# A hybrid decoder block on one core: low parts of weights, transposes and head copies given to other places

## The chip, the cores and the metric

The kernel runs on one core of one Trainium2 chip. The metric is the device time of one execution in microseconds (us). TensorE is called PE (PEld where it loads weights), VectorE DVE, ScalarE ACT, GpSimd POOL, SyncE SP. A `q` behind an engine's name (ACTq, SPq) is that engine's queue of DMA issues and semaphore instructions.

## What is computed

One layer for 512 tokens of width 1024, all in float32:

```python
h = rmsnorm(x, norm1_g);  proj = h @ w_in
u, v_g, q, k, v, q_idx, k_idx, w_idx, gates = split_cols(proj, IN_SIZES)
y_a = sgu_mixer(gelu(u), gelu(v_g), w_s, b_s, sgu_ln_g, sgu_ln_b)   # chunked gMLP
q, k, q_idx, k_idx = apply_rope(...)
y_b = dsa_attention(q, k, v, q_idx, k_idx, w_idx)  # 128 best keys of each query, 8 heads
merged = sigmoid(g0) * (y_a @ w_out_a) + sigmoid(g1) * (y_b @ w_out_b)
x = x + merged @ w_o
x = x + square(relu(rmsnorm(x, norm2_g) @ w_ff_in)) @ w_ff_out
return rmsnorm(x, norm_f_g)
```

The gMLP multiplies `u` by a spatially mixed, layer-normed `v_g`; the product is what the code holds in `u` after line 562, and its transpose `yaT` is the input of `y_a @ w_out_a`.

## The kernel before, in words

**Split products.** Each float32 matmul is three matmuls in a faster format: every operand is kept as a rounded high part and a low part (the rest). `split` (line 50) makes them: ACT writes the high part (line 51), and DVE, or the engine handed in, subtracts (line 52). A step of `gemm` (line 140) is one 128-row slice of the contraction: low weight by high input, high by low, high by high (lines 146 to 148).

**Weights** come in tiles of 128x1024 through `w_load` (line 102; issued from ACT's queue, two raw buffers `wr`) and `w_conv` (line 109), which makes `wh` on ACT and `wl` on the engine in `lo_eng["e"]`, three buffers each, and then issues the load of the next tile. That issue has to wait until both parts of an earlier tile have been made, since they free the raw buffer. `w_ahead(n)` is called after the first step of weight tile n and converts up to tile n+2. `lo_eng["e"]` is POOL from line 316 on and DVE again from line 529 on.

**Order.** The program writes TensorE's work as generators: a list `todo` of gemms, from which `fill(n)` takes n steps and which it places among the work of the other branches; what has to be done with a finished sum is put off by `later` to the next `tick`. A planner of the framework then orders each engine's queue by its own estimate of when operands are ready, with the program's order as priority; instructions within `tc.keep_in_program_order` keep their place. So most of the order is the program's, and some is the planner's.

**The stages around the change.** DVE searches the 128 best keys (lines 517 to 521: 16 rounds of MAX8 and MATCH_REPLACE8 over three score tiles) and after that makes masks (line 526). Below this, PE runs gate sums `ga`, and then the projection of the keys of heads 0 to 3 (`k`, tiles W_K0, 16 steps, line 551). Between its steps stand the four spatial mixes `sg` (lines 559 to 561), of which DVE makes the gated product `u` (line 562, one instruction for each of the four groups). Then comes the projection of the queries of heads 0 to 3 (`q`, tiles W_Q0, 16 steps, line 565), and after each of the first four of its steps one group of four transposes of `u` (line 570), which ACT copies (line 571) and DVE subtracts from (line 572) to `yaT` high and low. Then `oa`, the product with `w_out_a` (line 581, 30 steps by `fill(30)`), and then the heads.

**Head copies.** `rope` (line 328) turns the `k` or `q` sums by eight DVE instructions in all (lines 333 to 336) and two ACT copies. `k_done` and `q_done` (lines 541, 546) then call `restack` (line 349), which copies 32-row pieces to the layout of each of four heads `hh`: 32 copies for the keys, 16 for the queries, 64 KB each, all issued from SP's queue. A second round of the same copies serves heads 4 to 7 (lines 697, 698). Attention runs through `Block.scores` (lines 620, 621, tile `at`), `normalise`, `transpose` (tile `pt`) and `values` (tile `pv`), with `fill` putting steps of other sums between. The buffers `kq` of heads 2 and 3 are used again by heads 6 and 7.

Of the kernel before, what the change touches and what calls it, by code (L numbers as in the profile page):

```python
# [15 lines left out]
P = 128  # L16
# [17 lines left out]
def hybrid_block_kernel(ctx: ExitStack, tc: tile.TileContext, A: dict, out: bass.AP):  # L34
    nc = tc.nc
    ACT, DVE, POOL, PE = nc.scalar, nc.vector, nc.gpsimd, nc.tensor
# [7 lines left out]
    def bank(name, tag="ps"):  # L44
        return ps.tile([P, 512], F32, tag=tag, bufs=4, name=name)

    def f32(ap):
        return ap.bitcast(F32)
# [6 lines left out]
    def unit(tag, dt, name):  # L55
        bufs = dict(kq=6, T=3)[tag]
        return E.tile([P, 2, S], dt, tag=tag, bufs=bufs, name=name)
# [11 lines left out]
    def tick():  # L69
        for d in due:  # L70
            d[0] -= 1
        while due and due[0][0] <= 0:
            due.pop(0)[1]()
# [4 lines left out]
    def fill(n):  # L78
        while n > 0 and todo:
            try:  # L80
                next(todo[0])
                n -= 1
                tick()
            except StopIteration:
                todo.pop(0)
# [14 lines left out]
    lo_eng = dict(e=DVE)  # L100
# [39 lines left out]
    def gemm(dst, get, ah, al, evac, lag=1, t0=0):  # L140

        wh, wl, n = get()
        K = len(ah)
        for k in range(K):
            bh, bl = ah[k][:, t0:], al[k][:, t0:]
            PE.matmul(dst, wl[:, k], bh, start=(k == 0), stop=False)  # L146
            PE.matmul(dst, wh[:, k], bl, start=False, stop=False)  # L147
            PE.matmul(dst, wh[:, k], bh, start=False, stop=(k == K - 1))  # L148
            if k == 0 and n is not None:
                w_ahead(n)  # L150
            if k == K - 1:
                later(evac, lag)
            yield
# [35 lines left out]
    ident = G.tile([P, P], F32, name="ident")  # L189
# [138 lines left out]
    def rope(xy, T, name, t0):  # L328


        for n in range(2):
            a, b = tmp(f"{name}_a{n}")[:, t0:], tmp(f"{name}_b{n}")[:, t0:]
            DVE.tensor_tensor(a, xy[n], cosR[:, t0:], op=ALU.mult)
            DVE.tensor_tensor(b, xy[1 - n], sinR[:, t0:], op=ALU.mult)
            DVE.tensor_tensor(a, a, b, op=ALU.subtract if n == 0 else ALU.add)
            split(T[n], T[2 + n], a)

    def rope_tiles(gets, name, done, t0=0):
        xy = [bank(f"{name}{n}")[:, t0:] for n in range(2)]

        def finish():
            t = [unit("T", FR, f"{name}_T{c}") for c in range(2)]
            T = [t[c][:, d, t0:] for c in range(2) for d in range(2)]
            rope(xy, T, name, t0)
            done(T)
        for n in range(2):
            yield from gemm(xy[n], gets[n], hTh, hTl, finish if n else (lambda: None), t0=t0)

    def restack(dst, T, hh, order):
        for c, o in enumerate(order):  # L350
            nc.sync.dma_start(f32(dst[32 * c:32 * c + 32, :]), f32(T[o][32 * hh:32 * hh + 32, :]))

    def bcast_r():
        pr = bank("pr", "pa")
# [8 lines left out]
    def qi_done(T):  # L363
        for hh in range(4):
            if hh % 2 == 0:
                un = unit("kq", FR, f"QSi{len(QSi)}")
            q = un[:, hh % 2, :S - P]
            restack(q, T, hh, (0, 1, 2, 3))
            QSi.append(q)
# [25 lines left out]
    for n in range(2):  # L395
        b = bank(f"kti{n}", "pa")
# [7 lines left out]
    u, vg = None, None  # L404
# [121 lines left out]
        DVE.tensor_scalar(sc[i], sc[i], TAKEN, -BIG, op0=ALU.is_gt, op1=ALU.mult)  # L526
    while todo:
        fill(8)
    lo_eng["e"] = DVE


    kq = []

    def new_kq():
        kq.clear()
        for hp in range(2):
            un = [unit("kq", FR, f"kq{hp}{c}") for c in range(3)]
            kq.append((un[0][:, 0], un[0][:, 1], un[2][:, 0]))
            kq.append((un[1][:, 0], un[1][:, 1], un[2][:, 1]))

    def k_done(T):
        for hh in range(4):
            restack(kq[hh][1], T, hh, (0, 1, 0, 1))
            restack(kq[hh][2], T, hh, (2, 3, 2, 3))

    def q_done(T):
        for hh in range(4):
            restack(kq[hh][0], T, hh, (0, 1, 2, 3))

    new_kq()  # L550
    todo.append(rope_tiles(W_K0, "k0", k_done))
    fill(12)
    u = dst_uv["u"]
    vgh, vgl = vghl
    yaT = [half("ybt", 2, f"yaT{c}") for c in "hl"]
    for g in range(4):
        b = bank(f"sg{g}", "pa")
        c = slice(g * P, (g + 1) * P)
# [4 lines left out]
                                 u[:, :, c], op0=ALU.add, op1=ALU.mult)  # L563
    fill(4)
    todo.append(rope_tiles(W_Q0, "q0", q_done))
    for g in range(4):
        fill(1)
        b = bank(f"yt{g}", "pa")
        for c in range(NT):
            PE.transpose(b[:, c * P:(c + 1) * P], u[:, c, g * P:(g + 1) * P], ident)  # L570
        ACT.activation(yaT[0][:, g], b, AF.Copy)
        DVE.tensor_tensor(yaT[1][:, g], b, f32(yaT[0][:, g]), op=ALU.subtract)
    while todo:
# [121 lines left out]
    new_kq()  # L695
    flush()
    k_done(ybs["KT"])
    todo.append(rope_tiles(W_Q1, "q1", q_done))
    todo.extend(gate_b(m) for m in range(2, KD))
    fill(27)  # L700
# [433 lines left out]
```

## Time and profile before

| | |
|---|---|
| time, median of 3 runs | 706.39 us (706.03 to 706.98) |
| profiled execution: its own time, its span | 707.55 us, 705.8 us |
| granted TensorE clock, mean | 0.993 |
| busy: PE, PEld | 690.5 us (98%), 578.0 us (82%) |
| busy: DVE, ACT, POOL | 563.0 us (80%), 331.9 us (47%), 67.9 us (10%) |
| instructions | 8976 |

The profile is one execution. Times in it are counted from the start of the span. Busy time of PE is modelled, as matmuls are pipelined: a matmul of 128x512 is shown with 0.39 us, though the next one starts some 0.23 us after it. "Idle before" is what an engine stood still before an instruction, and an arrow names what it waited for.

### The profile page before, as it was taken

The numbers are of one execution on the slowest core, as the hardware profiler recorded it, in microseconds if no ns is written. First come the engines' busy times: TensorE is split into PE (matmuls) and PEld (weight loads), VectorE is DVE, ScalarE is ACT, GpSimd is POOL, SyncE is SP. The second block draws the span as 40 slices with busy tenths as digits, with TensorE's granted clock in tenths as the row PEclk, the third lists the DMA queues.
The fourth block names the chain that finished last, engine by engine and source line by source line (L and its number), as shares of the span: only waits on it lengthen the run. The fifth ranks groups of instructions, "written<-read, shape, count | busy, mean of one in ns | idle before, by whom it ended". The sixth has DMA issues, their size and how long they took to land.

```text
span 705.8 us, 8976 instructions
## 1 busy us (share of the span) xinstructions
PE 690.5 (98%) x3242; PEld 578.0 (82%) x3242; DVE 563.0 (80%) x1036; ACT 331.9 (47%) x572; POOL 67.9 (10%) x49
## 2 busy tenths in 40 slices
PE   9999999996999999999999999999999999999996
PEld 8998888885888887878888888888888888888885
DVE  5674999999557887768542978979798997979996
ACT  6644634413235546563335766445253544535234
POOL 0044348720000000000000000000000000000001
PEclk9999999998999999999999999999999999999999
DMA  9736222313652454214443223242323214233023
GB/s 328 264 95 190 60 90 90 108 42 113 183 155 75 136 143 124 75 46 141 158 154 133 74 99 129 69 150 90 120 92 116 92 59 150 90 119 114 7 61 119
DMA packets 27356, 82.03 MB, mean 116 GB/s; under 512 B 4656, under 2 KB 6320, under 8 KB 25264
## 3 DMA queue, kind: packets, MB, share of 16 engines
q10 hardware_dynamic: 14976, 60.34, 26.6%
q1 hardware_dynamic: 12336, 21.12, 9.5%
q8 instruction: 25, 0.41, 0.2%
q14 instruction: 19, 0.16, 0.1%
HBM read 71.48 MB, written 2.10 MB: 104 GB/s over the span
## 4 chain that ended last, share of the span: by engine, by line
PE 71%; DVE 3%; DMA 1%; SPq 1%; issue 1%; ACT 0%; POOLq 0%; POOL 0%; DVEq 0%; ACTq 0%
PE f L146 8%; PE f L147 8%; PE f L148 8%; PE pp L897 6%; PE pp L898 6%; PE pp L899 6%; PE wo L147 2%; PE wo L148 2%; PE wo L146 2%; PE gb L146 1%; PE gb L148 1%; PE gb L147 1%; PE pv L651 1%; PE pt L639 1%; PE q L146 1%; PE oa L147 1%
## 5 line engine op out<-in xcount | busy, mean ns | idle before, releaser
L51 ACT ACTIVATE wh<-wr 128x1024 fp32r<-128x1024 f32 x88 | 93.0, 1057 | 116.1 <-PE f L148 39.4
L52 DVE TENSOR_TENSOR wl<-wr,wh 128x1024 fp32r<-128x1024 f32 x69 | 83.9, 1218 | 21.4 <-ACT wh L51 19.8
L146 PE MATMUL f<-h2h,wl 128*128 128x512 f32 x256 | 100.1, 391 | 0.0
L147 PE MATMUL f<-h2l,wh 128*128 128x512 f32 x256 | 99.7, 390 | 0.0
L148 PE MATMUL f<-h2h,wh 128*128 128x512 f32 x256 | 99.7, 390 | 0.0
L51 ACT ACTIVATE u<-w2r 128x512 fp32r<-128x512 f32 x98 | 59.2, 624 | 75.0 <-DVE w2r L825 25.6
L899 PE MATMUL pp<-u,fp 128*128 128x512 f32 x196 | 76.2, 389 | 0.0
L898 PE MATMUL pp<-u,fp 128*128 128x512 f32 x196 | 76.2, 389 | 0.0
L897 PE MATMUL pp<-u,fp 128*128 128x512 f32 x196 | 71.9, 389 | 0.0
L910 DVE TENSOR_TENSOR P<-pp,P 128x512 f32<-128x512 f32 x84 | 54.4, 681 | 17.5 <-PE pp L899 17.5
L52 DVE TENSOR_TENSOR u<-w2r,u 128x512 fp32r<-128x512 f32 x98 | 64.3, 681 | 4.5 <-ACT u L51 4.4
L148 PEld LDWEIGHTS f<-h2h,wh 128*128 128x128 f32 x256 | 48.1, 188 | 10.0
L146 PEld LDWEIGHTS f<-h2h,wl 128*128 128x128 f32 x256 | 48.1, 188 | 9.8
L147 PEld LDWEIGHTS f<-h2l,wh 128*128 128x128 f32 x256 | 48.1, 188 | 9.7
L52 POOL TENSOR_TENSOR wl<-wr,wh 128x1024 fp32r<-128x1024 f32 x19 | 47.8, 2513 | 45.9 <-ACT wh L51 44.1
L899 PEld LDWEIGHTS pp<-u,fp 128*128 128x128 f32 x196 | 36.8, 188 | 7.7
L897 PEld LDWEIGHTS pp<-u,fp 128*128 128x128 f32 x196 | 36.8, 188 | 7.7
L898 PEld LDWEIGHTS pp<-u,fp 128*128 128x128 f32 x196 | 36.8, 188 | 7.6
L991 POOL TENSOR_TENSOR fss<-fss,mhalf 128x1 f32<-128x1 f32 x3 | 1.6, 547 | 313.8 <-DVE fss L990 313.8
L51 ACT ACTIVATE fp<-fs 128x256 fp32r<-128x256 f32 (+1 forms) x28 | 17.6, 629 | 29.6 <-DVE fs L875 17.0
L853 DVE SCALAR_TENSOR_TENSOR fr<-f,R 128x512 f32<-128x512 f32 x32 | 21.8, 684 | 10.2 <-PE f L148 8.3
L146 PE MATMUL gb<-hTh,wl 128*128 128x512 f32 x64 | 25.7, 401 | 0.0
(266 smaller groups left out, 1578.9 us busy)
## 6 DMA issues: line engine op xcount, KB each, us to landing
wr<-in_f ACTq DMA_DIRECT2D x36, 512.0 KB, 3.5
w2r<-in_f2p ACTq DMA_DIRECT2D x14, 1024.0 KB, 4.9
wr<-in_wt ACTq DMA_DIRECT2D x26, 512.0 KB, 3.6
wr<-in_wuv ACTq DMA_DIRECT2D x8, 512.0 KB, 3.9
kq<-k_T SPq DMA_DIRECT2D x64, 64.0 KB, 3.1
wr<-in_wo ACTq DMA_DIRECT2D x8, 512.0 KB, 3.5
xn<-in_xn SPq DMA_DIRECT2D x2, 1024.0 KB, 8.1
wr<-in_woa ACTq DMA_DIRECT2D x4, 512.0 KB, 3.8
```

Of the source, the lines that this page charges most:

```text
L51: ACT.activation(hi, src, AF.Copy)
L52: (eng or DVE).tensor_tensor(lo, src, f32(hi), op=ALU.subtract)
L146: PE.matmul(dst, wl[:, k], bh, start=(k == 0), stop=False)
L147: PE.matmul(dst, wh[:, k], bl, start=False, stop=False)
L148: PE.matmul(dst, wh[:, k], bh, start=False, stop=(k == K - 1))
L639: PE.transpose(b[:, j * P:(j + 1) * P], self.p[:, j * P:(j + 1) * P], ident)
L651: PE.matmul(b[:, s0 * P:], VS[j][:, h], rhs, start=(n == 0 and j == 0), stop=(n == 1 and j == NT - 1))
L853: DVE.scalar_tensor_tensor(r, b, 0.0, R2, op0=ALU.max, op1=ALU.mult)
L897: PE.matmul(b[j], fl, u[:, 0], start=(q == 0), stop=False)
L898: PE.matmul(b[j], fh, u[:, 1], start=False, stop=False)
L899: PE.matmul(b[j], fh, u[:, 0], start=False, stop=(q == 1))
L910: DVE.tensor_tensor(sums[name, j], b[j], sums[name, j], op=ALU.add)
```

## The change

The low parts of the weights stay on POOL until after the first 11 steps of `q`; DVE takes over there. The 16 transposes of the gated product move behind these 11 steps, and are held in the program's order. The copies of heads 2 and 3 (and so of heads 6 and 7) are issued by POOL, those of heads 0 and 1 (4 and 5) by SP as before.

```diff
-    def restack(dst, T, hh, order):
+    def restack(dst, T, hh, order, eng=nc.sync):
         for c, o in enumerate(order):
-            nc.sync.dma_start(f32(dst[32 * c:32 * c + 32, :]), f32(T[o][32 * hh:32 * hh + 32, :]))
+            eng.dma_start(f32(dst[32 * c:32 * c + 32, :]), f32(T[o][32 * hh:32 * hh + 32, :]))
...
     while todo:
         fill(8)
-    lo_eng["e"] = DVE
...
     kq = []
+    QUEUE = (nc.sync, nc.sync, nc.gpsimd, nc.gpsimd)
...
     def k_done(T):
         for hh in range(4):
-            restack(kq[hh][1], T, hh, (0, 1, 0, 1))
-            restack(kq[hh][2], T, hh, (2, 3, 2, 3))
+            restack(kq[hh][1], T, hh, (0, 1, 0, 1), QUEUE[hh])
+            restack(kq[hh][2], T, hh, (2, 3, 2, 3), QUEUE[hh])
 
     def q_done(T):
         for hh in range(4):
-            restack(kq[hh][0], T, hh, (0, 1, 2, 3))
+            restack(kq[hh][0], T, hh, (0, 1, 2, 3), QUEUE[hh])
...
     todo.append(rope_tiles(W_Q0, "q0", q_done))
+    fill(11)
+    lo_eng["e"] = DVE
     for g in range(4):
         fill(1)
         b = bank(f"yt{g}", "pa")
         for c in range(NT):
-            PE.transpose(b[:, c * P:(c + 1) * P], u[:, c, g * P:(g + 1) * P], ident)
+            tc.keep_in_program_order(PE.transpose(b[:, c * P:(c + 1) * P], u[:, c, g * P:(g + 1) * P], ident))
```

## Rows read from the trace of the kernel before

**Rows 1.** The page: busy us of each engine (share) xinstructions; the chain by engine.

```profile
PE 690.5 (98%) x3242; PEld 578.0 (82%) x3242; DVE 563.0 (80%) x1036; ACT 331.9 (47%) x572; POOL 67.9 (10%) x49
...
PE 71%; DVE 3%; DMA 1%; SPq 1%; issue 1%; ACT 0%; POOLq 0%; POOL 0%; DVEq 0%; ACTq 0%
```

**Rows 2.** Waits of PE, whole span: us in total, times, longest.

```profile
PE q L146 <- DVE wl L52: 3.8, 1, 3.8
PE yt L570 <- DVE u L562: 2.5, 1, 2.5
...
PE at L620 <- DMA kq<-q_T: 0.9, 1, 0.9
```

**Rows 3.** Timeline of PE: start, duration, instruction, [idle before <- releaser].

```profile
158.47 0.39 PE L148 MATMUL k<-hTh,wh 128*128 128x512 f32 x1
162.64 0.50 PE L146 MATMUL q<-hTh,wl 128*128 128x512 f32 x1 [3.78 <-DVE wl L52]
...
166.14 1.12 PE L570 MATMUL yt<-ident,u 128*128 128x128 f32 x4 [2.54 <-DVE u L562]
...
171.74 0.60 PE L570 MATMUL yt<-ident,u 128*128 128x128 f32 x4
172.09 0.48 PE L146 MATMUL q<-hTh,wl 128*128 128x512 f32 x1
...
180.36 0.39 PE L146 MATMUL oa<-yaTh,wl 128*128 128x512 f32 x1
```

**Rows 4.** Stretches of 1 us: busy us by engine, then clock (PEclk), DMA share, GB/s.

```profile
164.00:165.00 1.00, 0.00 (x0) 0.00 (x0) 0.80 (x1) 0.11 (x1) 0.00 (x0) 0.50 0.60 225
...
171.00:172.00 1.00, 1.00 (x8) 0.81 (x7) 1.00 (x2) 0.60 (x1) 0.00 (x0) 1.00 0.25 61
```

**Rows 5.** Timeline of DVE behind the key search.

```profile
160.56 0.89 DVE L526 TENSOR_SCALAR sc<-sc 128x384 f32<-128x384 f32 x3
161.37 1.22 DVE L52 TENSOR_TENSOR wl<-wr,wh 128x1024 fp32r<-128x1024 f32 x1
...
165.34 2.72 DVE L562 SCALAR_TENSOR_TENSOR u<-sg,lnt,u 128x512 f32<-128x512 f32 x4
...
169.17 0.68 DVE L335 TENSOR_TENSOR k_a<-k_a,k_b 128x512 f32<-128x512 f32 x1
```

**Rows 6.** Timeline of ACT and its DMA issues, the same stretch.

```profile
162.62 0.33 ACTq L106 DMA_DIRECT2D wr<-in_woa  x1
163.05 1.06 ACT L51 ACTIVATE wh<-wr 128x1024 fp32r<-128x1024 f32 x1 [15.12 <-DVE wl L52]
```

**Rows 7.** Groups and lines: mean ns, or duration ns min/median/max, of one.

```profile
L52 POOL TENSOR_TENSOR wl<-wr,wh 128x1024 fp32r<-128x1024 f32 x19 | 47.8, 2513 | 45.9 <-ACT wh L51 44.1 <-issue 1.8
...
L510 DVE TENSOR_TENSOR vg<-vg,lnt x4: 665/2283/2286, 108.6 to 137.2; 128x512 f32<-128x512 f32 x4
...
L519 DVE MAX8 m<-sc x48: 401/540/684, 85.1 to 158.7; 128x8 f32<-128x512 f32 x16, 128x8 f32<-128x384 f32 x16, 128x8 f32<-128x256 f32 x16
```

**Rows 8.** SP's issues of head copies by time; last row: KB each, us to landing.

```profile
170.54 23.16 SPq L351 DMA_DIRECT2D kq<-k_T  x32
193.80 13.20 SPq L351 DMA_DIRECT2D kq<-q_T  x16
233.89 23.27 SPq L351 DMA_DIRECT2D kq<-k_T  x32
...
kq<-q_T SPq DMA_DIRECT2D x18, 64.0 KB, 3.6
```

**Rows 9.** Timeline of PE: first scores of head 0, last of 3, first of 5 and 6.

```profile
200.99 0.28 PE L620 MATMUL at<-kq,kq 128*128 128x256 f32 x1
...
246.31 0.47 PE L620 MATMUL at<-kq,kq 128*128 128x512 f32 x1
...
268.81 0.35 PE L620 MATMUL at<-kq,kq 128*128 128x256 f32 x1 [0.91 <-DMA kq<-q_T]
...
278.03 0.28 PE L620 MATMUL at<-kq,kq 128*128 128x256 f32 x1
```

## The prediction

> **What bounds the kernel now.** I read the page first. PE is shown busy for 98% of the span and holds 71% of the chain that ended last; no other engine holds over 3% [rows 1]. So a microsecond is worth something only where PE stands still, or where its clock is low. Next I read the waits of PE. Behind the start-up there are few: 3.8 us for a low weight part made by DVE, 2.5 us for the gated product made by DVE, and 0.9 us for a copy of queries [rows 2]. The timeline of PE puts the first two side by side: the key projection's last matmul issues at 158.47, the first of `q` at 162.64, the first transpose at 166.14, and `oa` begins at 180.36 [rows 3]. [...] Last come the timelines of DVE and ACT: DVE is in its key search and masks up to 161.45, and only then (161.37, as starts overlap a little) gets to the low part that PE wants and to `u` (165.34) [rows 5]. ACT had nothing to do for 15.12 us, because the load issue of 162.62 stood at the head of its queue and waited for that low part to free the raw buffer [rows 6]. PE, ACT and the loads all waited for DVE.
>
> **What the stretch would take undisturbed.** The `k` sums end in issue slots at 158.70 (158.47 plus one slot of 0.23). From 172.09 to 180.36 PE does 12 `q` steps of three matmuls, 0.689 us each; a group of four transposes takes 0.35 (171.74 to 172.09) [rows 3]. Sixteen steps and four groups are 11.0 + 1.4 = 12.4 us. The trace has 180.36 - 158.70 = 21.7 us. So 9.2 us can be won: 3.8 + 2.5 of waits, and the other 2.9 is the low clock.
>
> **Part 1, low parts on POOL for longer.** Four low parts change engine: the two of `q` and the first two of `w_out_a`. DVE loses two of 1.22 us ahead of `u` (161.37 and its like at 164.20) [rows 5] and two later; POOL gains four of 2.51 us [rows 7]. ACT had the first high part ready when its idle time began, 163.05 - 15.12 = 147.9 [rows 6]. POOL needs 2.5 us from there: 150.4 in place of 162.6. The next load then issues, the second high part takes 1.06, POOL another 2.5: about 154.3. PE wants these at 158.70 and, eight steps later, at 164.2, so the first wait goes entirely. The third and fourth can start only when a buffer of high parts comes free, after `k` (158.7) and after the eighth step (164.2): with 1.06 on ACT and 2.51 on POOL they are there at 162.3 and 167.8, while `oa` begins at 171.1 and takes its second tile 5 us later. New waits: the load issues in ACT's queue now wait for POOL until 162.3 and 167.8, and the ACT copies of `yaT` and of the keys stand behind them; the first transposed group comes at 167.3, so this costs half a microsecond at most, which is inside the next term.
>
> Does POOL's work slow DVE? MAX8 has 401 to 684 ns for its three sizes through a search in which POOL was converting: no. But `L510`, which takes two SBUF inputs, took 665 ns once and 2283 ns at the median [rows 7]: 1.6 us lost each time that it met a conversion. [...]
>
> **Part 2, transposes behind 11 steps.** DVE is free of masks at 161.45. `u` takes 2.72 for all four [rows 5], so it is done by 164.2, or 164.9 with one rope instruction before it; the first transposes now come after 12 steps, at 158.70 + 8.3 = 167.0. The second wait goes, with 2 us to spare, and with no standstill I expect no low clock. What is late next is `yaT`: there are now only one `q` step and three `oa` steps between the last transposes and the matmul that reads their low part, at 171.1 + 3 x 0.689 + 0.2 = 173.4. Until then DVE has, from 161.45, `u` 2.72, eight rope instructions and four low parts of `yaT` at about 0.68 (line 335's time [rows 5]): 2.7 + 5.4 + 2.7 = 10.9, to 172.3. That leaves 1.1 us. With no block PE does not wait; with one block of 1.6 it waits 0.5, with two 2.1. I take one: 0.5. Ends: 0 and 2.1.
>
> **Part 3, half of the copies on POOL.** In the trace SP issues 32 key copies in 23.2 us (0.72 each), then 16 query copies in 13.2 (0.83 each), which land 3.6 us later [rows 8]. The first scores stand at 200.99 [rows 9]; they would be wanted 9.2 earlier, at 191.8. With one queue the head-0 queries would not be there: key copies from about 168.1 (170.54 less two low parts of DVE) or 171.3 with two blocks, 23.2 for the keys, 3.3 for four queries, 3.6 to land, that is 198.2 to 201.4. With SP carrying heads 0 and 1 alone: 11.6 in place of 23.2, so 186.6 to 189.8, ahead of 191.8. So this part wins little by itself, but without it the others' win would be lost. In the second round the 0.9 us wait at 268.81 is for head 5's queries, behind 32 key copies [rows 9]; SP has 16 fewer ahead of them: 0.9 won (bounds 0 and 0.9).
>
> POOL's issue of a copy is nowhere in the trace. Bounds: SP's pace of 0.72 [rows 8], and 2.51 for POOL's longest instruction [rows 7]. It is the same copy through another queue, so it is nearest to SP's row: I take 0.72. The tight place is the second round: head 6 uses buffers that head 3's last scores (246.31, done 246.8) set free, and its own scores come at 278.03 [rows 9]: 31.2 us, less the 0.9, less 3.6 for landing, 26.7 us for 12 key and 4 query copies, 1.67 each. At 0.72 there is no wait. Behind the copies in POOL's queue are only two memsets, which nobody needs before the heads' first `values`.
>
> **The sum**: -9.2 - 0.9 + 0.5 = -9.6 us. On the profiled execution (span 705.8, own time 707.55) that is 696.2 and 697.9; its own time is 1.2 above the median of 706.39, from which I count: 696.8 us.
>
> **Rivals.**
> *A new wait takes the old one's place.* `oa` waits for `yaT` the full 2.1 us, and the clock falls again (2.9 us, as before). For it: DVE has no idle time up to there. Against: 3.8 us of standstill came before the fall in the trace, and this is shorter. Time: 706.39 - 9.2 + 2.1 + 2.9 = 702.2.
> *The change does not do what it says for the heads.* If two queues share one pace, the copies arrive as late as with one: a wait of 6.4 to 9.6 us at the first scores, 8.0 in the middle, and the 0.9 stays. For it: the first scores stood at the edge already. Against: SP's queue is shown issuing one after the other. Time: 706.39 - 9.2 + 0.5 + 8.0 = 705.7.
> *Slower: POOL's copies bind in the second round.* At 2.51 each, 16 take 40.2 in place of 26.7; PE stands still for 13.5 us ahead of head 6: 706.39 - 9.6 + 13.5 = 710.3. It turns the change into a loss above (26.7 + 9.6) / 16 = 2.3 us each. For it: POOL is the slow engine in every row that it shares with DVE. Against: nothing in the rows makes an issue cost as much as subtracting 1024 columns.
> [...]
>
> **How the numbers follow.** Forecast 0.68, new wait 0.13, heads late 0.07, POOL's copies 0.09; 0.03 for orders of the planner that I can't see. A measurement of this kernel tells about 0.2%, 1.4 us, from no change. Faster: 0.68 + 0.13 + 0.01 = 0.82. Same: the third case and 0.01, 0.08. Slower: 0.10. Range: the best sum is 706.39 - 9.2 - 0.9 = 696.3, less the 1.0 by which the three runs differ: 695.3. Above, it takes in the first rival with 0.8 for the runs: 703.0. That leaves out 0.19. The forecast's own part of it ends at 706.39 - 9.2 + 2.1 = 699.3.
>
> **What would show it.** Right: no wait of PE for `wl` or `u` between 158 and 172, clock 1.00 throughout, `oa` beginning near 171, first scores near 192 without a wait, key copies in two queues, POOL's conversions at 148 to 155 inside the key search. Wrong: a wait of PE at `oa` for `yaT`; one at `at` for a copy, and then whether its head is 0 (SP) or 2, 3, 6, 7 (POOL); rope instructions of over 2 us; a stretch at clock 0.50 in another place. If `oa` begins near 171 and the time still doesn't fall by 8 us, what was won was given back in the heads.

## The result and the profile after

| | before | after |
|---|---|---|
| median | 706.21 us (705.22 to 706.98, 4 runs) | 702.55 us (701.96 to 702.67, 4 runs) |
| profiled execution: own time, span | 707.55, 705.8 us | 702.48, 700.8 us |
| granted TensorE clock, mean | 0.993 | 0.994 |

The ratio is 0.9947 [0.993, 0.9964]: faster, by 3.7 us where 9.6 were forecast. Lines of the changed kernel stand up to two further down than before: the transposes are line 572, the copies of `yaT` on ACT line 573, its low parts line 574, the memsets of `ptl` and its twin 606 and 607.

The page after, busy time and the chain of work (answers to [rows 1]):

```profile
PE 689.8 (98%) x3242; PEld 578.6 (83%) x3242; DVE 560.9 (80%) x1032; ACT 332.2 (47%) x572; POOL 101.4 (14%) x101
...
PE 97%; issue 1%; POOL 0%; DVE 0%; ACT 0%; POOLq 0%
```

POOL has four conversions and 48 copies more; the chain now runs through PE alone for 97%. The waits of PE (answers to [rows 2]):

```profile
PE oa L146 <- issue: 2.8, 1, 2.8
```

The three waits of [rows 2] are gone, and one of 2.8 us at `oa` is new ("issue" is what the view prints when it can name no releaser). The timeline of PE (answers to [rows 3] and [rows 9]):

```profile
166.50 0.60 PE L572 MATMUL yt<-ident,u 128*128 128x128 f32 x4
...
174.03 0.76 PE L146 MATMUL oa<-yaTh,wl 128*128 128x512 f32 x1 [2.82 <-issue]
...
197.59 0.28 PE L622 MATMUL at<-kq,kq 128*128 128x256 f32 x1
```

The first transposes issue at 166.50 without a wait (forecast 167.0). `oa` begins at 174.03 instead of 180.36, which is 6.3 us won, but its 30 steps then take 197.59 - 174.03 = 23.56 us, where before they took 200.99 - 180.36 = 20.63. The stretches of 1 us tell why (answers to [rows 4]: length, then busy us of PE, PEld, DVE, ACT and POOL with instructions, then clock, DMA share, GB/s):

```profile
173.00:174.00 1.00, 0.00 (x0) 0.00 (x1) 0.04 (x1) 0.67 (x2) 1.00 (x2) 0.70 0.50 127
174.00:175.00 1.00, 0.97 (x2) 0.58 (x3) 1.00 (x2) 1.00 (x3) 1.00 (x3) 0.50 0.35 47
...
180.00:181.00 1.00, 1.00 (x5) 0.87 (x4) 1.00 (x2) 0.24 (x1) 1.00 (x3) 0.88 1.08 236
181.00:182.00 1.00, 1.00 (x6) 0.81 (x6) 0.17 (x1) 0.39 (x1) 1.00 (x3) 1.00 1.13 234
```

The granted clock falls to 0.50 late in the standstill (0.70 in the stretch from 173, 0.50 in those from 174 to 179, 0.88 in that from 180) and is back at 1.00 from 181: the 2.9 us by which the steps of `oa` take longer are this. So 2.8 + 2.9 = 5.7 us were given back of the 9.2 + 0.9 that were to be won: 4.4 are left, against 3.7 measured.

Where does the wait come from? The timeline of POOL after:

```profile
146.87 2.40 POOL L52 TENSOR_TENSOR wl<-wr,wh 128x1024 fp32r<-128x1024 f32 x1
...
151.57 2.40 POOL L52 TENSOR_TENSOR wl<-wr,wh 128x1024 fp32r<-128x1024 f32 x1 [2.30 <-ACT wh L51]
...
164.39 0.20 POOL L607 MEMSET ptl<- 128x128 f32 x1 [8.34 <-DVE u L562]
164.56 2.39 POOL L52 TENSOR_TENSOR wl<-wr,wh 128x1024 fp32r<-128x1024 f32 x1
170.57 2.35 POOL L52 TENSOR_TENSOR wl<-wr,wh 128x1024 fp32r<-128x1024 f32 x1 [3.62 <-issue]
172.86 4.14 POOL L351 DMA_DIRECT2D kq<-k_T  x8
```

And that of ACT with its DMA issues (answers to [rows 6]):

```profile
166.98 0.33 ACTq L106 DMA_DIRECT2D wr<-in_woa  x1
167.53 0.63 ACT L51 ACTIVATE k_T<-k_a 128x512 fp32r<-128x512 f32 x1 [7.93 <-DVE k_a L335]
168.86 0.63 ACT L51 ACTIVATE k_T<-k_a 128x512 fp32r<-128x512 f32 x1 [0.69 <-DVE k_a L335]
169.40 1.04 ACT L51 ACTIVATE wh<-wr 128x1024 fp32r<-128x1024 f32 x1
172.95 0.33 ACTq L106 DMA_DIRECT2D wr<-in_woa  x1
173.33 2.07 ACT L573 ACTIVATE yaTh<-yt 128x512 fp32r<-128x512 f32 x4 [2.89 <-POOL wl L52]
```

Read the two together as one chain. A memset stands ahead of the third conversion in POOL's queue and waits 8.34 us for `u`, so the conversion ends at 166.95. ACT's load issue, which waits for it, goes at 166.98, the two key copies after it as DVE's rope delivers them, and only then, at 169.40, the fourth high part. POOL makes its low part from 170.57 to 172.92. The next load issue waits for that (172.95), and behind the issue stand the four copies of `yaT`, the first of them free to go since the transposes of 166.5: they run at 173.33, and `oa` at 174.03. Last, the timeline of DVE (answers to [rows 5]):

```profile
160.21 0.89 DVE L526 TENSOR_SCALAR sc<-sc 128x384 f32<-128x384 f32 x3
...
161.61 2.72 DVE L562 SCALAR_TENSOR_TENSOR u<-sg,lnt,u 128x512 f32<-128x512 f32 x4
...
165.44 2.06 DVE L335 TENSOR_TENSOR k_a<-k_a,k_b 128x512 f32<-128x512 f32 x1
...
173.96 2.48 DVE L574 TENSOR_TENSOR yaTl<-yt,yaTh 128x512 fp32r<-128x512 f32 x4 [3.15 <-ACT yaTh L573]
```

The one block that the prediction took is there (2.06 instead of 0.68 us, beside the third conversion), but DVE stood idle for 3.15 us ahead of the low parts of `yaT`: it was waiting for ACT. The head copies issued by POOL, by line (ns of one, min/median/max), and SP's issues by time (answer to [rows 8]):

```profile
L351 POOL DMA_DIRECT2D kq<-k_T x32: 496/496/758, 172.9 to 249.6; - x32
```

```profile
168.19 11.92 SPq L351 DMA_DIRECT2D kq<-k_T  x16
180.21 9.08 SPq L351 DMA_DIRECT2D kq<-q_T  x8
```

POOL issues a copy in 0.50 us (the first eight in 4.14), SP beside it at a pace of 11.92 / 16 = 0.75, and no matmul waits for one.

### The profile page after: what moved, and what is told of

Its sections match the earlier page's. It is cut to its first block, busy times and chain, and to the rows that moved or that the text cites. A ratio compares the mean times of both kernels' runs of the same rounds, so it can differ in the third digit from the quotient of the medians.

```text
span 700.8 us, 8998 instructions
## 1 busy us (share of the span) xinstructions
PE 689.8 (98%) x3242; PEld 578.6 (83%) x3242; DVE 560.9 (80%) x1032; ACT 332.2 (47%) x572; POOL 101.4 (14%) x101
## 3 DMA queue, kind: packets, MB, share of 16 engines
q0 software_dynamic: 1536, 3.15, 1.8%
## 4 chain that ended last, share of the span: by engine, by line
PE 97%; issue 1%; POOL 0%; DVE 0%; ACT 0%; POOLq 0%
PE f L146 8%; PE f L148 8%; PE f L147 8%; PE pp L901 6%; PE pp L899 6%; PE pp L900 6%; PE va L283 4%; PE gb L147 2%; PE gb L146 2%; PE gb L148 2%; PE wo L147 2%; PE wo L146 2%; PE ga L147 2%; PE ga L146 2%; PE wo L148 2%; PE ga L148 2%
## 5 line engine op out<-in xcount | busy, mean ns | idle before, releaser
L52 DVE TENSOR_TENSOR wl<-wr,wh 128x1024 fp32r<-128x1024 f32 x65 | 79.1, 1219 | 19.5 <-ACT wh L51 19.3
L52 POOL TENSOR_TENSOR wl<-wr,wh 128x1024 fp32r<-128x1024 f32 x23 | 57.3, 2490 | 51.6 <-ACT wh L51 46.2
L521 DVE MATCH_REPLACE8 sc<-m,sc 128x512 f32<-128x512 f32 (+2 forms) x48 | 25.5, 537 | 0.0
```

What stands on the lines that cost most here:

```text
L52: (eng or DVE).tensor_tensor(lo, src, f32(hi), op=ALU.subtract)
L521: DVE.match_replace(out=sc[i], in_to_replace=m8[i], in_values=sc[i], imm_value=TAKEN)
```

## The experiments

Two theories for the 5.7 us. **T1, the memset**: the third conversion is late because of the memset ahead of it; with that gone the whole chain moves forward. The rival, **ACT's queue**: whatever makes POOL late, `oa` waits only because a load issue that waits for POOL stands ahead of the copies of `yaT`; with that issue elsewhere POOL may be late. The expectations number them otherwise: Theory 1 there is T1, Theory 2 is that POOL's conversions are too slow as such for the load issues that wait for them on ACT, and Theory 3 that DVE is behind with `yaT`. Each ratio is to the kernel before, run beside it on the same chip.

**The memsets off POOL** (e1).

```diff
-    POOL.memset(f32(pth[:, 11]), 0.0)
-    POOL.memset(f32(ptl[:, 11]), 0.0)
+    DVE.memset(f32(pth[:, 11]), 0.0)
+    DVE.memset(f32(ptl[:, 11]), 0.0)
```

> The two memsets of the transposed weights' zero blocks go from POOL to DVE; nothing else moves in any queue. Theory 1 (queue heads): in the changed kernel the second memset stood ahead of the third conversion in POOL's queue and waited until 164.4 for the gated product, which put the third conversion at 164.6 and, through the load issue in ACT's queue, the fourth at 170.6 and the copies of yaT at 173.3. Without it the third should begin near 159.7 and the fourth, behind the two key copies in ACT's queue, near 169; yaT near 172 and oa near 172.5 in place of 174.0, so 1.5 us for the wait and up to 2.9 more if the clock stays up: 698 to 701 us against 702.5. Theory 2 (POOL's conversions are too slow as such for the load issues that wait for them on ACT): oa stays near 174, 702.5 us. Theory 3 (DVE is behind with yaT): no change either.

Measured: 702.86 us (702.38 to 703.62), ratio 0.9955 [0.9941, 0.9968], which is the changed kernel's time. The timelines of POOL, of DVE, of ACT and of PE:

```profile
160.27 2.40 POOL L52 TENSOR_TENSOR wl<-wr,wh 128x1024 fp32r<-128x1024 f32 x1 [5.76 <-ACT wh L51]
171.75 2.34 POOL L52 TENSOR_TENSOR wl<-wr,wh 128x1024 fp32r<-128x1024 f32 x1 [9.08 <-issue]
```

```profile
160.74 2.68 DVE L526 TENSOR_SCALAR sc<-sc 128x384 f32<-128x384 f32 x3
```

```profile
168.71 0.63 ACT L51 ACTIVATE k_T<-k_a 128x512 fp32r<-128x512 f32 x1 [8.57 <-DVE k_a L335]
...
170.58 1.04 ACT L51 ACTIVATE wh<-wr 128x1024 fp32r<-128x1024 f32 x1
174.12 0.33 ACTq L106 DMA_DIRECT2D wr<-in_woa  x1
174.50 2.07 ACT L573 ACTIVATE yaTh<-yt 128x512 fp32r<-128x512 f32 x4 [2.88 <-POOL wl L52]
```

```profile
175.20 0.77 PE L146 MATMUL oa<-yaTh,wl 128*128 128x512 f32 x1 [3.45 <-issue]
```

The third conversion does start 4.3 us earlier, and nothing is won. It now meets DVE's three masks, which take 2.68 instead of 0.89 us; the rope instructions begin later by that, and though none of them is held up now, ACT's key copies come 1.2 us later (168.71 instead of 167.53), and the fourth high part stands behind these copies either way. The wait is even longer. T1 has fallen: the memset is a link of the chain, and removing it puts another in its place.

**The loads off ACT** (e2): in the stretch where POOL converts, POOL issues the next load too, behind its own conversion.

```diff
-    lo_eng = dict(e=DVE)
+    lo_eng, ld_eng = dict(e=DVE), dict(e=nc.scalar)
...
-            w_load()
+            w_load(ld_eng["e"])
...
     while todo:
         fill(8)
+    ld_eng["e"] = POOL
...
     fill(11)
-    lo_eng["e"] = DVE
+    lo_eng["e"], ld_eng["e"] = DVE, nc.scalar
```

> The loads that wait for POOL's conversions are issued by POOL itself, behind each conversion, instead of by ACT; the memsets stay where they are. Theory 1: the third and fourth conversions stay late (164.6 and about 170.5), but nothing stands ahead of the yaT copies on ACT any more than the fourth high part, done at 170.4: yaT from 170.5, oa between 171.0 and 171.6 with no fall of the clock, 697 us. Theory 2: the same, as it also takes the wait out of ACT's queue. Theory 3: oa still waits 2 to 3 us, for the low parts of yaT, 702 us.

Measured: 698.17 us (698.03 to 698.99), ratio 0.989 [0.9877, 0.9904]. `oa` begins at 171.82; PE:

```profile
171.82 0.47 PE L146 MATMUL oa<-yaTh,wl 128*128 128x512 f32 x1 [0.47 <-issue]
```

A second wait of 0.21 us for the low part of `yaT` follows, the clock is 1.00 in every stretch from 170 to 176, and the first scores stand at 192.84. This is what ACT's queue as the cause asks for, and not what Theory 3 gave (702 us): DVE was not the bound. It moved several issues, so it does not say yet which of them counts; the ninth experiment does.

**Both** (e3: the two diffs together).

> Memsets on DVE and the loads issued by POOL. Theory 1: the fourth high part is done near 169 and oa begins at 171.0 without a wait: 697 us, the same as with the loads alone within 0.5. Theory 2 the same. Theory 3: 702 us.

Measured: 698.95 us (698.54 to 699.29), ratio 0.9899 [0.9885, 0.9912]. The memsets' move adds nothing here either: the masks take 2.63 us again, `oa` begins at 172.38, with waits of 1.05 and 0.20. The stretch behind them tells something of the clock:

```profile
173.00:174.00 1.00, 0.94 (x4) 0.82 (x5) 1.00 (x3) 1.00 (x3) 1.00 (x1) 1.00 0.51 129
```

After a standstill of 1.05 us the clock stayed at 1.00, in every stretch up to 176.

**Two conversions on POOL instead of four** (e4).

```diff
     todo.append(rope_tiles(W_Q0, "q0", q_done))
-    fill(11)
     lo_eng["e"] = DVE
+    fill(11)
```

> DVE takes the low parts back before the 11 steps of q instead of behind them: POOL makes two (both of q), DVE the two of w_out_a; the memsets stay on POOL. Theory 1: no conversion stands behind the memset, and the load issues on ACT wait for DVE only: oa begins between 171.0 and 171.8, 697 to 698 us. Theory 2: the same. Theory 3 (DVE is the bound): two more conversions of 1.2 us on DVE make it worse, oa at 174 to 176, 703 to 706 us.

Measured: 699.7 us (699.31 to 701.16), ratio 0.9913 [0.9901, 0.9926]. The profiled execution is the longest of the five; its timelines of ACT and PE, and one of its stretches:

```profile
172.38 0.33 ACTq L106 DMA_DIRECT2D wr<-in_woa  x1
172.76 2.07 ACT L573 ACTIVATE yaTh<-yt 128x512 fp32r<-128x512 f32 x4 [1.73 <-DVE wl L52]
```

```profile
173.41 0.51 PE L146 MATMUL oa<-yaTh,wl 128*128 128x512 f32 x1 [1.82 <-ACT yaTh L573]
```

```profile
175.00:176.00 1.00, 1.00 (x4) 0.72 (x3) 1.00 (x3) 0.76 (x1) 1.00 (x3) 0.50 0.97 385
```

The load issue now waits for DVE's low part, and the copies of `yaT` stand behind it all the same. DVE is sooner than POOL (its low part takes 1.23 us, from 171.12, where POOL's took 2.35), so the wait is 1.82 us instead of 2.82, and here too the clock falls (0.62, 0.50, 0.50 and 0.67 in the stretches from 174 to 178). That need not be so in each execution: the mean granted clock is 0.996 in this one, and 0.998 in three of the others, as in e9 below, which has no fall. POOL's slowness is a part of the size of the wait; that there is one is the issue's doing, as e9 shows.

**One queue for the head copies** (e5: e2's kernel with part 3 taken back).

```diff
-    QUEUE = (nc.sync, nc.sync, nc.gpsimd, nc.gpsimd)
+    QUEUE = (nc.sync,) * 4
```

> As e2 (loads issued by POOL), but all head copies from SP's queue again, so that the split of the copies is taken out while the stretch ahead is short. Theory A (without the split the copies give the gain back): key copies begin at 168.3 as in e2, 23.2 us for 32 of them, 3.3 for four queries and 3.6 to land give 198.4, while PE comes to the first scores at 192.8: a wait of 5 to 6 us, with a fall of the clock behind it up to 3 more: 703.5 to 707 us against 698.2. Theory B (the copies were never in the way): 698 to 699 us.

Measured: 702.1 us median, of four runs that lie far apart (699.11, 701.0, 703.2, 703.45), ratio 0.995 [0.9931, 0.997]. The profiled one is the 699.11:

```profile
193.56 0.36 PE L622 MATMUL at<-kq,kq 128*128 128x256 f32 x1 [0.60 <-DMA kq<-q_T]
```

Only 0.60 us is lost there, not 6.4 to 9.6. SP begins at 168.28, at the early end of the prediction's bounds, but issues 32 key copies in 21.11 us instead of 23.2 and 16 query copies in 10.71 instead of 13.2, and the scores are wanted at 193.0 rather than 191.8. The same kernel was profiled once more (e12):

> A second profile of e5 (one copy queue, loads by POOL): its profiled run took 699.1 us, three others 701.0 to 703.5. If the difference is the copies' landing, a run of 701 to 703 us shows a wait of 2 to 5 us at the first scores of head 0 for the query copies, with or without a fall of the clock; a run near 699 shows 0.6 again.

Measured: 699.78 us; the wait at the same place is 1.21 us:

```profile
194.21 0.36 PE L622 MATMUL at<-kq,kq 128*128 128x256 f32 x1 [1.21 <-DMA kq<-q_T]
```

So with the waits gone one queue is at the edge, and both profiles lose about a microsecond to it. These two are the shortest of the five executions, though. By the medians one queue costs 702.1 - 698.17 = 3.9 us against e2, between what the two theories gave, and the intervals of the two ratios do not touch. What took 2 to 4 us more in the three runs without a profile stays open; the two longest have a mean granted clock of 0.996 and 0.995 instead of 0.998, which would fit a longer wait with a fall of the clock behind it, but this is not shown.

**Part 3 alone** (e6: the kernel before with the copies split between SP and POOL as in the change).

```diff
+    QUEUE = (nc.sync, nc.sync, nc.gpsimd, nc.gpsimd)
```

> The kernel before with the split of the head copies alone. Theory A: the only wait of PE for a copy (0.9 us, second round) goes, and perhaps the 0.4 us of the same stage's end; the two waits and the low clock around 160 to 171 stay: 704.8 to 706.1 us against 706.1. Theory B, that copies from POOL cost something (its queue, DVE): 707 us or more.

Measured: 705.47 us (704.35 to 706.78, 10 runs), ratio 0.9992 [0.9983, 1.0002]: not told from no change. The waits of 3.79 and 2.09 us and the low clock (0.50 from 164 to 168) are all there; the 0.9 us wait at the scores is not.

**Part 2 alone** (e7: the kernel before with the transposes behind 11 steps and held in order).

```diff
     todo.append(rope_tiles(W_Q0, "q0", q_done))
+    fill(11)
...
-            PE.transpose(b[:, c * P:(c + 1) * P], u[:, c, g * P:(g + 1) * P], ident)
+            tc.keep_in_program_order(PE.transpose(b[:, c * P:(c + 1) * P], u[:, c, g * P:(g + 1) * P], ident))
```

> The kernel before with the transposes behind 11 steps alone; low parts on DVE, one copy queue. The first wait (3.8 us for the low part) and the fall of the clock behind it stay, the second (2.5 us for u) goes; the copies of one queue land near 200.6, PE comes to the first scores near 198.5: about 2 us are given back there. 704 to 706 us. If the clock doesn't fall, 3 us less at the stretch, all of it given back at the copies: the same.

Measured: 703.56 us (702.91 to 704.15), ratio 0.9962 [0.9949, 0.9975].

The wait for `u` is gone, that for the low part stays (3.78 us), and the clock falls here too (0.77 in the 2 us from 160, 0.50 from 162 to 166, 0.52 in the 2 us from 166). `oa` begins at 178.10. The 2 us that were expected to be given back at the copies are not: the first scores stand at 198.73 without a wait, so the time lies below the expected range.

**Part 1 alone** (e8): the low parts on POOL, with the transposes where they were.

```diff
     while todo:
         fill(8)
-    lo_eng["e"] = DVE
...
         DVE.tensor_tensor(yaT[1][:, g], b, f32(yaT[0][:, g]), op=ALU.subtract)
+    fill(7)
+    lo_eng["e"] = DVE
```

> The kernel before with the low parts on POOL until 11 steps of q alone; transposes after the first four steps, one copy queue. The first wait goes; the first transposes come at 159.4 and wait for u until 162.4, 3 us, long enough for the clock to fall as it did; the rest of the stretch as in the kernel before. The copies start 2 us earlier and land near 198, PE comes to the first scores between 195 and 198: 701 to 704 us. If the load issues behind POOL hold up yaT here too, it shows less, as yaT has 12 steps until oa.

Measured: 702.41 us (701.3 to 702.69), ratio 0.9945 [0.993, 0.996].

```profile
162.65 0.66 PE L569 MATMUL yt<-ident,u 128*128 128x128 f32 x4 [3.23 <-DVE u L561]
```

(In this kernel the transposes are line 569 and `u` line 561.) The first wait is gone, the second longer (3.23 instead of 2.54 us), the clock is 0.50 from 164 to 167, and `oa` begins at 176.36. The copies of `yaT` are not late, as their transposes come four steps into `q`. The parts alone win 3.6, 2.4 and 0.5 us; together they win 3.7. Part 1 and part 2 alone each leave one standstill of over 3 us (3.23 and 3.78) with a fall of the clock to 0.50 behind it, so their gains need not add up; and together they run into the wait at `oa`, which neither e7 nor e8 has.

**One issue moved** (e9): the kernel after, with a single load issue, the one behind the fourth conversion, given to POOL; the issues of the first three loads stay with ACT, and the memset stays where it is.

```diff
-    fill(11)
-    lo_eng["e"] = DVE
+    fill(8); ld_eng["e"] = POOL; fill(3)
+    lo_eng["e"], ld_eng["e"] = DVE, nc.scalar
```

> The changed kernel with one DMA issue moved: the load behind the fourth conversion is issued by POOL instead of ACT; every other queue is the same instruction for instruction. Theory Q (the one issue at the head of ACT's queue costs all that is missing): yaT is copied from 171.0 in place of 173.3, right behind the fourth high part, oa begins near 171.7, the clock stays at 1.00, 698 us as in e2. Theory R (the loads ahead of it matter too): between 699 and 702 us.

Measured: 697.26 us (696.99 to 697.74), ratio 0.9869 [0.9852, 0.9885]; span 695.8. The timelines of ACT, POOL and PE:

```profile
169.85 1.04 ACT L51 ACTIVATE wh<-wr 128x1024 fp32r<-128x1024 f32 x1
170.80 2.04 ACT L573 ACTIVATE yaTh<-yt 128x512 fp32r<-128x512 f32 x4
```

```profile
164.84 0.21 POOL L607 MEMSET ptl<- 128x128 f32 x1 [8.33 <-DVE u L562]
165.01 2.40 POOL L52 TENSOR_TENSOR wl<-wr,wh 128x1024 fp32r<-128x1024 f32 x1
171.03 2.40 POOL L52 TENSOR_TENSOR wl<-wr,wh 128x1024 fp32r<-128x1024 f32 x1 [3.62 <-issue]
173.74 0.75 POOL L106 DMA_DIRECT2D wr<-in_woa  x1 [0.31 <-POOL wl L52]
```

```profile
171.51 0.44 PE L146 MATMUL oa<-yaTh,wl 128*128 128x512 f32 x1
172.16 0.50 PE L147 MATMUL oa<-yaTl,wh 128*128 128x512 f32 x1 [0.21 <-DVE yaTl L574]
...
192.46 0.28 PE L622 MATMUL at<-kq,kq 128*128 128x256 f32 x1
```

The stretch behind the wait:

```profile
173.00:174.00 1.00, 1.00 (x6) 0.84 (x5) 1.00 (x3) 0.79 (x1) 0.69 (x2) 1.00 0.25 66
```

POOL is as late as in the kernel after, or later by half a microsecond: memset, third and fourth conversion all stand where they stood. But ACT goes on to `yaT` right behind the fourth high part, PE waits 0.21 us in all from the last steps of `k` to the first scores, the clock is 1.00 in every stretch from 158 to 185, and `oa` runs from 171.51 to the first scores at 192.46. One issue in another queue is worth 5.3 us against the changed kernel's 702.55, measured in another comparison. This settles the cause of the wait at `oa`, and the version beats both kernels.

**The third low part on DVE** (e10: e2's kernel, POOL converting all but the third).

```diff
-    fill(11)
+    lo_eng["e"] = DVE
+    fill(4)
+    lo_eng["e"] = POOL
+    fill(7)
     lo_eng["e"], ld_eng["e"] = DVE, nc.scalar
```

> As e2 (loads issued by POOL), with the third low part on DVE and only the fourth on POOL behind the search, so that no conversion of POOL meets the masks or the rope. If the 0.5 us at oa left in e2 comes from DVE being held up by the third conversion (a rope instruction of 2.06 us there): no rope instruction over 0.7 us, yaT copied from about 169.5, oa at 171.2 without a wait, 697.2 to 697.8 us. If 1.2 us more on DVE cost as much as the block: 698.2 us, no change.

Measured: 697.84 us (697.65 to 698.26), ratio 0.9878 [0.9863, 0.9893], not told from e2's or e9's. The rope instruction is not held up any more:

```profile
165.51 0.68 DVE L335 TENSOR_TENSOR k_a<-k_a,k_b 128x512 f32<-128x512 f32 x1
```

`oa` begins at 171.27 and waits 0.23. So the block on DVE is real and costs the kernel nothing that can be measured, once ACT's queue is free.

**The kernel before once more** (e11: a second profile of it).

> A second profile of the kernel before, as its first was 1.4 us over the median of its runs. Expected: the same two waits (3.8 and 2.1 to 2.5 us) and a stretch at clock 0.50; its span 1 to 2 us under 705.8, the difference in the length of that stretch or in the 0.9 us wait for a copy.

Measured: 706.77 us, span 705.1. The waits of PE:

```profile
PE q L146 <- DVE wl L52: 3.8, 1, 3.8
PE yt L570 <- DVE u L562: 1.9, 1, 1.9
```

The 3.8 is the same; that for `u` is 1.9 instead of 2.5, and further down the list there is no wait at the scores at all. So the first is in both profiles of this kernel (and in those of e6 and e7), and the 0.9 is in one of the two. The span is only 0.7 us under 705.8, not 1 to 2: behind the same 3.78 us the clock is low for longer here (0.76 in the 2 us from 160, 0.50 from 162 to 170, 0.68 in the 2 us from 170; in the first profile 0.94 in the stretch from 163, 0.50 from 164 to 170, 0.64 in that from 170).

## Why the prediction was right and wrong

**Right: what could be won.** "So 9.2 us can be won: 3.8 + 2.5 of waits, and the other 2.9 is the low clock." The low clock is in the trace: 0.50 in the stretches from 164 to 169, 0.64 in that from 170, 1.00 from 171 (both ends in [rows 4]); at 2.9 us it is what the waits leave of the 9.2. The kernel with one more issue moved gets 706.53 - 697.26 = 9.3 us, its first scores at 192.46 against the forecast 191.8, and its time is within half a microsecond of the forecast 696.8. In the changed kernel the first two conversions end at 149.3 and 154.0 (forecast 150.4 and 154.3), and `q` and the transposes start without a wait. The first is a microsecond early because the forecast counted from 147.9, the start of ACT's idle time, and POOL took up the high part at 146.87.

**Wrong: the step on the new waits of part 1**, "the load issues in ACT's queue now wait for POOL until 162.3 and 167.8, and the ACT copies of `yaT` and of the keys stand behind them [...] so this costs half a microsecond at most, which is inside the next term". It named the queue and who stands in it; its times were wrong. It let the third and fourth conversion start as soon as a buffer of high parts came free. In the trace the third ends at 166.95 and the fourth at 172.92, 4.7 and 5.1 us later. The third was behind a memset that the prediction had placed behind the copies, harmless there; the fourth's high part was behind the key copies in ACT's queue, which the first issue and DVE's rope held up. Of what was ahead of these two in their own queues the step counted nothing. In its place stands a wait of 2.8 us instead of 0.5, and e9 shows that it hangs on the second of these issues alone.

**Wrong: "with no standstill I expect no low clock".** There was a standstill of 2.82 us, and behind it the clock was 0.50 in every stretch from 174 to 179. The rival of the new wait gave 702.2, close to the 702.55 measured, but its 2.1 us were to come from blocks on DVE, and the trace has DVE idle there, waiting for ACT. That the size came out was luck. The reason held against it, that 3.8 us had come before the fall in the trace, showed only that 3.8 is enough, not that less isn't.

**The 0.9 of the second round** is the doubtful term, and may be what the sum of -4.4 has too much: e11 is without it, and part 3 alone is at -0.5 with an interval that holds zero.

**Part 2's term** of 0.5 for a block on DVE: that a rope instruction would be held up once was the author's estimate from the 1.6 us of `L510`, and no run shows the 0.5. The block came (2.06 instead of 0.68 us) and cost nothing that shows: in e9, with it, PE waits 0.21 us for the low part of `yaT`, in e10, without it, 0.23.

**Part 3's price**: 0.72 us each was taken with 2.51 as the upper end; 0.50 was measured, so the slower rival had no ground. A copy issued by POOL lands 3.6 to 3.8 us after its issue (medians for queries and keys), and the next one issues after 0.50. The rival of one shared pace is out as well: the two queues ran beside each other (SP's 16 key copies from 168.19 to 180.11, POOL's first eight from 172.86 to 177.00). That without the split "the others' win would be lost" was half right: by the medians of e5 and e2 one queue costs 3.9 of the 8 us, but not in the way it was worked out, as the two profiles show waits of 0.60 and 1.21 us instead of 6.4 to 9.6, with SP issuing faster than was taken.

## What to carry to other kernels

In these traces a DMA issue that waited for a semaphore stopped everything behind it in ACT's queue (2.89 us after the change, 1.73 in e4). So when a producer is moved to a slower engine, list what stands behind each issue that waits for that producer, and give the issue to the producer's own queue. When a moved instruction's start is worked out, go through its engine's queue, not its operands alone: the last wait ahead of it can set its start, as the memset's 8.34 us did for the third conversion. And a standstill of PE is priced with the clock behind it where the clock falls: 2.8 us cost 5.7 here.

## What the runs showed of the hardware that was not expected

**A waiting issue held ACT.** ACT stood idle for 2.89 us with four copies ready, since the issue at 172.95 waited for POOL. The price shows in e9, which gets 5.3 us by moving that one issue.

**Beside a conversion of POOL, masks with one input took three times as long.** The masks of line 526 read one tile and write it, and took 2.68 (e1) and 2.63 us (e3) beside a conversion instead of 0.89. The prediction had looked for this in instructions with two SBUF inputs alone, as `L510`. The key search's MAX8 is not held up: three took 1.47 us beside the conversion of 151.57 in the changed kernel and 1.48 without one (157.25).

**The clock fell behind shorter standstills than the 3.8 us of the trace before.** In the profiled executions it fell to 0.50 behind standstills of 3.78 (before), 3.45 (e1), 3.23 (e8), 2.82 (after) and 1.82 us (e4); behind 1.21 (e12), 1.05 (e3) and 0.47 us (e2) it stayed at 1.00. What lies between is not shown, and the length need not be all that counts: what PE had done before was not the same in each, and behind the same 3.78 us the clock is at 0.50 from 162 in e11 and from 164 in the first profile. At `oa` the fall cost 2.9 us.
